# A middle stage in the source's order: attention work as a plan of single-engine steps at set k-tiles

## The chip, the cores and the metric

The kernel runs on one core of a Trainium2 chip. Its engines are TensorE (PE; its weight loads are listed apart, as PEld), VectorE (DVE), ScalarE (ACT), GpSimd (POOL) and SyncE (SP, which here only issues DMAs). Each engine works through its own list of instructions in order and waits at semaphores for the others. The metric is the time of the whole kernel on the device, in microseconds, as a median of several runs.

## What is computed

One decoder layer on 256 tokens of width 4096, all in float32. The reference, cut:

```python
h = _rmsnorm(x, norm_g[l])
proj = h @ w_in[l]
(q_a, k_a, v_a, z_a, q_b, kc, vc, ksl, vsl, kwn, vwn, z_b, g_b) = jnp.split(proj, ...)
o_a = _dilated_mixture(heads(q_a, 16) * HEAD_DIM ** -0.5, heads(k_a, 16), heads(v_a, 16), slopes_a)
gates = jax.nn.sigmoid(g_b).reshape(B, S, N_HEADS_B, 3)
o_b = _nsa(heads(q_b, 16), ..., gates, slopes_b, cmp_k_pe[l], cmp_k_w1[l], ...)
y_a = _rmsnorm(o_a, out_g_a[l]) * jax.nn.silu(z_a)
y_b = _rmsnorm(o_b, out_g_b[l]) * jax.nn.silu(z_b)
x = x + jnp.concatenate([y_a, y_b], axis=-1) @ w_out[l]
return _rmsnorm(x, final_g)
```

Mixer A is a windowed attention with three dilations and an ALiBi penalty, 16 heads of 128. Mixer B is an attention with three gated branches (compressed, selected, window), 16 heads over two groups of keys and values; its compressed keys and values come from a small two-layer network (`_compress`).

## The kernel before

Float32 products are made from two parts of each factor: a high part (`wh`, `xh`) and the rest (`wl`, `xl`). `mm3` issues three matmuls for one product: high by high, low by high, high by low (lines 97, 98, 99). `split_to` makes the parts, the high one on ScalarE (line 104) and the low one on VectorE (line 105), which needs the high one first.

The kernel has five stages. A first stream of weight chunks (to about 205 us); then `run_pairs` over the chunks of q, k, v of mixer A and q of mixer B, which are evicted to DRAM by DMAs of GpSimd's queue (`scr_q`, `scr_k`, `scr_v`, `scr_qb`), to about 853 us; then the middle stage, which the change rewrites, to about 1361 us; then `run_pairs` over most of the output projection, and a last stream.

The middle stage is one call of `run_stream` over eight chunks of 512 columns: seven gate chunks (z of both mixers) and the first chunk of `w_out`. A chunk has 32 k-tiles of 128 rows, and a k-tile six matmuls of 512 columns into `acc`. A weight DMA brings four k-tiles (`w`); they are split in halves of two k-tiles, two halves ahead of the matmuls (`LOOK`). Beside this stream the attentions run as background tasks, generators in the list `tasks`: `attend_a` (four head groups of mixer A), `compress` (keys, then values), `mixer_done`, `start_b`, `attend_b` (four head groups, each in two halves of 128 queries, `attend_half`; the second half has twice the keys and is called the larger one here), later `turn_y` and `sum_y`. After each k-tile `run_stream` adds a pace of 1.45 (1.3 in the last chunk) to a credit, and for each whole credit `advance` runs one generator to its next yield; such a step may issue a whole chain across the engines. That settles only the order of the source: `ordered.close()` at line 357 leaves the manual schedule, so that the tile framework's scheduler orders each engine's instructions, and the stage of `run_pairs` afterwards enters it again (line 1341).

Names in the rows: `fetched` is a tile read back from DRAM (`fetch`, two buffers), `table` the ALiBi table of a head of mixer A (`load_table`, line 649, GpSimd's queue, three buffers), `cmat` the distances of mixer B. In mixer A, `s` are scores, `n` table minus scores, `mn` its minima, then the exponentials in `n`, `pt` transposes, `pah` and `pal` their parts, `po` the product with the values. In mixer B, `nb` holds a half's scores of four heads, `den` the denominators, which are inverted and multiplied by the gates (lines 1007 and 1009) and then into `nb` (line 1012, four heads); `turn` (line 1047) transposes a block of 128 keys of four heads into `pt`, which becomes `pbh` and `pbl`; `c` is the compressed branch; `oT` turns a half's result. `sz` are the gates z, with Silu on ScalarE. ScalarE loads a table when its function changes (ACT_TABLE_LOAD).

Of the kernel before, what the change touches and what calls it, by code (L numbers as in the profile page):

```python
# [82 lines left out]
def hybrid_trunk(ctx: ExitStack, tc: tile.TileContext, a: dict):  # L83
# [234 lines left out]
    def run_stream(begin=None, last=False, ordered=None):  # L318
# [6 lines left out]
        for i, (u, s) in enumerate(subs):  # L325
# [49 lines left out]
            for j in range(n):  # L375
                k = k0 + n * s + j
                for m in range(NT):
                    h, l = lhs(k, m)
                    mm3(ps[m][:, :width], h, l, wh[:, j], wl[:, j], start=(k == 0), stop=(k == KT - 1))
                if k == KT - 1:  # L380
                    done(ps)
                if (c, k) in hooks:
                    hooks[c, k]()
                credit = min(credit + pace * width / CW, 2.0)
                while credit >= 1.0 and tasks:
                    credit -= 1.0
                    advance()
# [201 lines left out]
    def split_values(src):  # L589

        v = room["work"].tile([P, NT, 4, 2, HD], F32R, name="va", tag="n", bufs=2)
        for m in range(NT):
            split_to(v[:, m, :, 0], v[:, m, :, 1], src[:, m].rearrange("p (j d) -> p j d", j=4))
        return v

    def transposed(src, key, scale=None):

        if key == "ka":
            hl = room["work"].tile([P, 2, 4, SEQ], F32R, name="kaT", tag="n", bufs=2)
            h, l = hl[:, 0], hl[:, 1]  # L600
        else:
            h = room["work"].tile([P, 4, SEQ], F32R, name=key + "Th", tag="qTh", bufs=1)
            l = room["work"].tile([P, 4, SEQ], F32R, name=key + "Tl", tag="qTl", bufs=1)
        for pair in range(2):
            pt = room["psm"].tile([P, 2, NT, P], F32, name="pt", tag="ps")
            for j in range(2):
                for m in range(NT):
                    hh = 2 * pair + j
                    nc.tensor.transpose(pt[:, j, m], src[:, m, hh * HD : (hh + 1) * HD], ident)
            split_to(h[:, 2 * pair : 2 * pair + 2].rearrange("p a b -> p (a b)"),  # L610
                     l[:, 2 * pair : 2 * pair + 2].rearrange("p a b -> p (a b)"),
                     pt.rearrange("p a b c -> p (a b c)"), scale)
            yield
        st[key + "T"] = (h, l)

# [13 lines left out]
    def split_psum(pt, n, nm):  # L629
        h = room["work"].tile([P, CW], F32R, name=nm + "h", tag="pTh", bufs=2)  # L630
        l = room["work"].tile([P, CW], F32R, name=nm + "l", tag="pTl", bufs=2)
        split_to(h[:, :n], l[:, :n], pt[:, :n])
        return h, l

    def pipeline(units, stages, at):

        for t in range(len(units) + at[-1]):
            for f, d in reversed(list(zip(stages, at))):
                if 0 <= t - d < len(units):
                    f(units[t - d])  # L640
            yield
            yield
# [8 lines left out]
    def attend_a(hg):  # L651
        vsrc, qsrc = st.pop("va"), st.pop("qa")
        v = split_values(vsrc)
        ksrc = fetch(f"k{hg}")
        yield
        yield from transposed(qsrc, "qa", SCALE)
        yield from transposed(ksrc, "ka")
        if hg == 1:
            st["kvc"] = fetch("kvc")
        elif hg < 3:  # L660
            st["va"], st["qa"] = fetch(f"v{hg + 1}"), fetch(f"q{hg + 1}")
        else:
            st["sel"], st["kw"] = fetch("sel"), fetch("kw", 2 * HD)
        qh, ql = st["qaT"]
        kh, kl = st["kaT"]
        o_tiles("a")
# [3 lines left out]
        def scores(j):  # L670
            s = room["psm"].tile([P, SPAN], F32, name="s", tag="ps")
            mm3(s[:, :P], qh[:, j, :P], ql[:, j, :P], kh[:, j, :P], kl[:, j, :P])
            mm3(s[:, P:], qh[:, j, P:], ql[:, j, P:], kh[:, j], kl[:, j])
            n = room["zq"].tile([P, SPAN], F32, name="n", tag="zt", bufs=4)
            head = hg * 4 + j
            nc.vector.tensor_sub(n, tables.pop(head), s)
            load_table(head + 2)
            mn = room["work"].tile([P, NT], F32, name="mn", tag="mn", bufs=4)
            den = room["work"].tile([P, NT], F32, name="den", tag="den", bufs=4)
            for m in range(NT):  # L680
                nc.vector.tensor_reduce(mn[:, m : m + 1], n[:, parts[m]], axis=AX.X, op=OP.min)
            for m in range(NT):
                nc.scalar.activation(n[:, parts[m]], n[:, parts[m]], AF.Exp, bias=mn[:, m : m + 1], scale=-1.0,
                                     accum_out=den[:, m : m + 1])
            rden = room["work"].tile([P, NT], F32, name="rden", tag="rden", bufs=4)
            nc.vector.reciprocal(rden, den)
            live[j] = (n, rden)

        def turn(j):
            n, rden = live[j]  # L690
            pt = room["psm"].tile([P, SPAN], F32, name="pt", tag="ps")
            for b in range(3):
                nc.tensor.transpose(pt[:, b * P : (b + 1) * P], n[:, b * P : (b + 1) * P], ident)
            live[j] = (*split_psum(pt, SPAN, "pa"), rden)

        def values(j):
            ph, pl, rden = live.pop(j)
            head = hg * 4 + j

            po = room["pso"].tile([P, NT, 2, HD], F32, name="po", tag="po")  # L700
            for m, blocks in enumerate([[(0, 0)], [(P, 0), (2 * P, 1)]]):
                out = po[:, m].rearrange("p s d -> p (s d)")
                for at, b in blocks:
                    vb = v[:, b, j].rearrange("p s d -> p (s d)")
                    nc.tensor.matmul(out, ph[:, at : at + P], vb, start=b == 0, stop=False)
                    nc.tensor.matmul(out, pl[:, at : at + P], vb, start=False, stop=b == m)
            oh = o_at("a", head * HD, HD)
            nc.scalar.activation(oh, po[:, :, 0], AF.Copy)
            nc.vector.tensor_add(oh, oh, po[:, :, 1])
# [3 lines left out]
        yield from pipeline(range(4), [scores, turn, values], [0, 1, 2])  # L713
        square_sums("a", hg)

    def square_sums(which, hg):
        for m in range(NT):
            junk = room["zq"].tile([P, CW], F32, name="junk", tag="zt", bufs=4)
            nc.scalar.activation(junk, o_at(which, hg * CW, CW)[:, m], AF.Square,
                                 accum_out=o_sb["ss" + which][:, m, hg : hg + 1])  # L720
# [11 lines left out]
    waiting, finished, gated = {"a": [], "b": []}, set(), set()  # L732

    def gate(which, i, sz=None):
        r = o_sb["r" + which]
        if sz is None:
            sz = []
            for m in range(NT):
                sz.append(room["zq"].tile([P, CW], F32, name="sz", tag="zt", bufs=4))
                nc.sync.dma_start(sz[m], scratch(f"z{which}{i}")[:, m])  # L740
            yield
            yield
# [677 lines left out]
```

## Time and profile before

| what | us |
|---|---|
| median of 3 runs | 1676.73 |
| lowest and highest | 1673.76, 1678.68 |
| the profiled execution | 1672.55 |
| its span in the trace | 1670.8 |
| TensorE busy in it | 1625.5 |
| TensorE's weight loads | 1340.3 |
| VectorE, ScalarE, GpSimd busy | 1330.9, 1016.3, 148.0 |

The mean granted clock of TensorE in this execution is 0.991. A row of the timeline has the start, the time of the instructions, engine and line, what is written and read, how many (x4), and in brackets the idle time of the engine before it with what ended it. Matmuls overlap, so that the time of one is longer than the distance of two.

### The profile page before, as it was taken

The page shows a single profiled execution, that of the slowest core. Times are in us where ns is not written, and L with a number is a line of the kernel's source. Part 1 is how long each engine was busy: PE and PEld are TensorE (multiplying, and loading weights), DVE is VectorE, ACT ScalarE, POOL GpSimd, SP SyncE. Part 2 cuts the span into 40 slices and gives each one's busy share as a digit, 9 for nine tenths or more (in the row PEclk, how much of TensorE's full clock was granted, in tenths as well). Part 3 has the DMA queues.
Part 4 walks back from the last instruction along what each step waited for, and adds up shares of the span by engine and source line. Part 5 has one row for each costly group of instructions (what it writes and reads, how often), then busy time and mean ns, then how long its engine had stood idle before and what let it go on. Part 6 is the DMA issues. An engine that isn't in the chain of part 4 may idle for free.

```text
span 1670.8 us, 20883 instructions
## 1 busy us (share of the span) xinstructions
PE 1625.5 (97%) x7772; PEld 1340.3 (80%) x7772; DVE 1330.9 (80%) x1446; ACT 1016.3 (61%) x1355; POOL 148.0 (9%) x203
## 2 busy tenths in 40 slices
PE   8999999999999999999978999999999999999997
PEld 5888978788888888888867877777888878878887
DVE  6586699989898998989846777876676859898984
ACT  6675556566656565656536757866666745656554
POOL 0000001111111110202030000000000000111110
PEclk9999999999999999999989999999999999999999
DMA  9785756979797888879796665534345456898974
GB/s 355 282 319 172 239 194 218 278 246 269 249 262 245 268 249 251 265 237 273 239 296 211 252 254 181 198 139 141 130 172 208 166 199 202 231 270 244 300 281 173
DMA packets 103542, 390.78 MB, mean 234 GB/s; under 512 B 12496, under 2 KB 13136, under 8 KB 90000
## 3 DMA queue, kind: packets, MB, share of 16 engines
q1 hardware_dynamic: 80064, 336.22, 57.3%
q0 software_dynamic: 22944, 52.18, 14.1%
q8 instruction: 61, 1.00, 0.2%
q10 hardware_dynamic: 432, 1.05, 0.2%
q14 instruction: 41, 0.34, 0.1%
HBM read 341.11 MB, written 50.38 MB: 234 GB/s over the span
## 4 chain that ended last, share of the span: by engine, by line
PE 86%; DVE 6%; DMA 3%; issue 3%; ACT 2%; POOL 0%; ACTq 0%; POOLq 0%; SPq 0%; DVEq 0%
PE p L98 14%; PE p L99 14%; PE p L97 14%; PE acc L98 11%; PE acc L99 10%; PE acc L97 10%; PE e L99 2%; PE e L97 2%; PE e L98 2%; DVE bf L458 2%; DMA scr_qb<-parts 1%; DMA w<-in_w_in 1%; PE pt L1047 1%; DVE bf L457 1%; DVE bt L451 1%
## 5 line engine op out<-in xcount | busy, mean ns | idle before, releaser
L105 DVE TENSOR_TENSOR wl<-w,wh 128x1024 fp32r<-128x1024 f32 (+2 forms) x210 | 247.2, 1180 | 147.7 <-ACT wh L104 144.9
L104 ACT ACTIVATE wh<-w 128x1024 fp32r<-128x1024 f32 (+2 forms) x210 | 214.1, 1023 | 140.4 <-PE acc L99 125.9
L97 PE MATMUL acc<-wh,xh 128*128 128x512 f32 (+2 forms) x768 | 294.2, 384 | 3.9 <-ACT wh L104 3.8
L98 PE MATMUL acc<-wl,xh 128*128 128x512 f32 (+2 forms) x768 | 291.9, 380 | 1.8 <-DVE wl L105 1.8
L99 PE MATMUL acc<-wh,xl 128*128 128x512 f32 (+2 forms) x768 | 291.1, 379 | 0.0
L458 DVE TENSOR_TENSOR bf<-bt,bf 128x2048 fp32r<-128x2048 f32 x99 | 226.2, 2284 | 0.0
L453 ACT ACTIVATE bf<-bt 128x1024 fp32r<-128x1024 f32 x99 | 104.9, 1060 | 163.2 <-DVE bt L451 163.1
L105 DVE TENSOR_TENSOR bp<-bw,bp 128x2048 fp32r<-128x2048 f32 x66 | 151.0, 2288 | 63.7 <-ACT bp L104 63.7
L450 ACT ACTIVATE bf<-bw 128x1536 fp32r<-128x1536 f32 x99 | 147.0, 1485 | 68.9 <-DMA bw<-in_w_in 46.7
L457 DVE TENSOR_TENSOR bf<-bw,bf 128x1536 fp32r<-128x1536 f32 x99 | 173.4, 1751 | 0.0
L104 ACT ACTIVATE bp<-bw 128x2048 fp32r<-128x2048 f32 x66 | 126.1, 1911 | 76.7 <-PE e L99 62.4
L97 PEld LDWEIGHTS acc<-wh,xh 128*128 128x128 f32 x768 | 145.4, 190 | 28.5 <-ACT wh L104 5.7
L98 PEld LDWEIGHTS acc<-wl,xh 128*128 128x128 f32 x768 | 145.9, 190 | 26.5 <-DVE wl L105 3.4
L99 PEld LDWEIGHTS acc<-wh,xl 128*128 128x128 f32 x768 | 145.4, 189 | 24.8
L456 ACT ACTIVATE bf<-bt 128x1024 fp32r<-128x1024 f32 x99 | 105.3, 1063 | 39.6 <-DVE bt L455 38.0
L451 DVE TENSOR_TENSOR bt<-bw 128x1024 f32<-128x1024 f32 x99 | 120.9, 1222 | 10.2 <-DMA bw<-in_w_in 7.0
L98 PE MATMUL p<-bf,sum 128*128 128x512 f32 x288 | 113.1, 393 | 2.6 <-DVE bf L458 2.5
L97 PE MATMUL p<-bf,sum 128*128 128x512 f32 x288 | 112.3, 390 | 0.0
L99 PE MATMUL p<-bf,sum 128*128 128x512 f32 x288 | 112.2, 390 | 0.0
L98 PE MATMUL p<-bp,xh 128*128 128x512 f32 x288 | 112.1, 389 | 0.0
L97 PE MATMUL p<-bp,xh 128*128 128x512 f32 x288 | 112.0, 389 | 0.0
L99 PE MATMUL p<-bp,xl 128*128 128x512 f32 x288 | 112.0, 389 | 0.0
(330 smaller groups left out, 3279.2 us busy)
## 6 DMA issues: line engine op xcount, KB each, us to landing
bw<-in_w_in SPq DMA_DIRECT2D x256, 512.0 KB, 6.4
w<-in_w_in SPq DMA_DIRECT2D x76, 1024.0 KB, 5.0
bw<-in_w_out SPq DMA_DIRECT2D x96, 512.0 KB, 5.4
w<-in_w_out SPq DMA_DIRECT2D x16, 1024.0 KB, 4.9
scr_q<-parts POOLq DMA_DIRECT2D x30, 256.0 KB, 7.7
scr_k<-parts POOLq DMA_DIRECT2D x30, 256.0 KB, 7.6
scr_v<-parts POOLq DMA_DIRECT2D x30, 256.0 KB, 7.7
scr_qb<-parts POOLq DMA_DIRECT2D x30, 256.0 KB, 7.5
```

The source lines that it names most:

```text
L97: nc.tensor.matmul(out, lh, rh, start=start, stop=False)
L98: nc.tensor.matmul(out, lh, rl, start=False, stop=False)
L99: nc.tensor.matmul(out, ll, rh, start=False, stop=stop)
L104: nc.scalar.activation(h, src, AF.Copy)
L105: nc.vector.tensor_sub(l, src, h.bitcast(F32))
L450: nc.scalar.activation(h[:, :3], w[:, B22:], AF.Copy)
L451: nc.vector.tensor_tensor(t[:, T3 : T1 + 1], w[:, B22 : B11 + 1], w[:, B12 : B12 + 1].to_broadcast([P, 2, CW]), op=OP.subtract)
L453: nc.scalar.activation(h[:, 3:5], t[:, T3 : T1 + 1], AF.Copy)
L456: nc.scalar.activation(h[:, 5:], t[:, T2:], AF.Copy)
L457: nc.vector.tensor_sub(l[:, :3], w[:, B22:], h[:, :3].bitcast(F32))
L458: nc.vector.tensor_sub(l[:, 3:], t, h[:, 3:].bitcast(F32))
L1047: nc.tensor.transpose(pt[:rows, j], src, ident)
```

## The change

The manual schedule is kept through the middle stage: `ordered` is no argument of `run_stream` any more, and each engine gets its instructions in the order in which the source issues them. The generators are replaced by a heap, `plan`, of steps with a time in k-tiles of the stage. Each step issues work for one engine mostly. `run_plan` runs after each k-tile what has become due.

```diff
@@ run_stream @@
-    def run_stream(begin=None, last=False, ordered=None):
+    def run_stream(begin=None, last=False):
...
             if i == 0 and begin:
                 begin()
-                if ordered:
-                    ordered.close()
...
                 if (c, k) in hooks:
                     hooks[c, k]()
+                clock[0] += width / CW
+                run_plan()
...
+    def at(time, f, *args):
+        heapq.heappush(plan, (time, len(planned), f, args))
+        planned.append(time)
...
+    def run_plan():
+        while plan and plan[0][0] <= clock[0]:
+            run_next()
...
     def load_table(head):
         if head < NH:
-            tables[head] = room["work"].tile([P, SPAN], F32, name="table", bufs=3)
-            nc.gpsimd.dma_start(tables[head], a["consts"][:, N_TAB + head * SPAN : N_TAB + (head + 1) * SPAN])
...
+            tables[head] = room["work"].tile([P, SPAN], F32, name="table", bufs=2)
+            nc.sync.dma_start(tables[head], a["consts"][:, N_TAB + head * SPAN : N_TAB + (head + 1) * SPAN])
...
+        plan_turns(when, q, 0, SCALE)
+        if hg == 0:
+            when(0, values_high, v)
+            when(1, values_low, v)
+            when(2, get, k)
+            when(3, get, following[0])
+            plan_turns(when, k, 8)
...
+        for j in range(4):
+            for d, f in enumerate((scores, maxima, weights, turn, high, low, values, first_half, both_halves, divide)):
+                when(t0 + 4 * j + d, f, j)
...
+    def plan_gates(when, which, t, *ids):
+        for n in range(0, len(ids), 2):
+            when(t, get_gates, which, *ids[n : n + 2])
+        for n, i in enumerate(ids):
+            when(t + 6, silu, which, i)
+            when(t + 7 + n, gate, which, i)
...
         for j in range(4):
+            for i in range(len(cuts)):
+                when(2 * j + i, scores, j, i)
+                when(2 * j + i + 1, distances, j, i)
+            when(2 * j + len(cuts), maxima, j)
+            when(2 * j + len(cuts) + 1, weights, j)
+        t = 8 + len(cuts)
...
+        when(t + 0.2, gate_weights)
+        for j in range(4):
+            when(t + 0.3 + 0.5 * (j // 2), weigh, j)
...
+        step = 2 if m else 3
+        t += 1.5
+        for i in range(len(blocks)):
+            for d, f in enumerate((turn, high, low, values)):
+                when(t + step * i + d, f, i)
...
         open_b()
+        get("v0")
+        get("q0")
+        load_table(0)
+        load_table(1)
         cmat = room["work"].tile([P, N_TAB], F32, name="cmat", bufs=1)
...
-        st["va"], st["qa"] = fetch("v0"), fetch("q0")
-        load_table(0)
-        load_table(1)
-        tasks.extend([attend_a(0), attend_a(1), compress(0), compress(1), attend_a(2), attend_a(3), mixer_done("a"), start_b()]
-                     + [attend_b(hg) for hg in range(4)] + [mixer_done("b")])
-
-    pace = 1.45
...
+        plan_attentions()
...
+                when(38, mixer_done, "a")
+                plan_gates(when, "a", 38, 0, 1, 2, 3)
...
+    RATE_A, RATE_C, RATE_B = 0.75, 0.6, 1.0
...
-    run_stream(begin_rest, ordered=ordered)
-    while tasks:
-        advance()
+    run_stream(begin_rest)
+    while plan:
+        run_next()
...
-    ordered.enter_context(tc.manual_schedule())
     rest = run_pairs(a["w_out"], dcs, y_lhs, y_sops, begin_out, OUT_PLACES, OUT_BANKS, out=True)
```

A rate turns steps into k-tiles: 0.75 for mixer A, 0.6 for the compression, 1.0 for mixer B. The compression takes keys and values together; head groups follow one another at fixed distances (a half of mixer B every 10 or 11 k-tiles). In mixer B the compressed block is now the last of a half. Gates of mixer A that were computed before their mixer was done come back for Silu in one go. The sums of y are planned 1.5 k-tiles apart in the last chunk.

Three places in the order of the instructions follow. The lines of the two kernels differ by the text that was added (`split_to` is at 104 and 105 before, at 105 and 106 now; `fetch` at 577 and 578).

GpSimd at the start of the stage, before: `scr_qb` are evictions of the last pairs, `c` the memset of the compressed weights' tile.

```order
L478 DMA scr_qb_5825<-parts 128x512 x2
L478 DMA scr_qb_5824<-parts 128x512 x2
L478 DMA scr_qb_5825<-parts 128x512
L1289 MEMSET c_5960 128x384
L649 DMA table<-in_consts 128x384 x11
```

SyncE at the same place, now: `w` are weights of the stage, `scr_v`, `scr_q` and `scr_k` the first head group's values, queries and keys.

```order
L274 DMA w<-in_w_in 128x2048 x3
L578 DMA fetched<-scr_v_3290 128x1024
L578 DMA fetched<-scr_q_2308 128x1024
L626 DMA table<-in_consts 128x384 x2
L1510 DMA cmat<-in_consts 128x800
L274 DMA w<-in_w_in 128x2048
L578 DMA fetched<-scr_k_2782 128x1024
```

The tables have moved from GpSimd's queue, behind the evictions, to SyncE's, between the fetches and `cmat`; two of them are issued at once.

TensorE at the first transposes (`pt<-ident,nb`) of the first larger half of mixer B, before:

```order
L97 MATMUL acc<-wh,xh_104 128x512
L98 MATMUL acc<-wl,xh_104 128x512
L99 MATMUL acc<-wh,xl_105 128x512
L1090 MATMUL pt<-ident,oT 128x128 x4
L1047 MATMUL pt<-ident,nb 128x128 x2
L97 MATMUL acc<-wh,xh_104 128x512 x2
L1047 MATMUL pt<-ident,nb 128x128 x2
L98 MATMUL acc<-wl,xh_104 128x512
L99 MATMUL acc<-wh,xl_105 128x512
```

TensorE at the same transposes, now:

```order
L98 MATMUL s<-kBh,qTh 128x272
L99 MATMUL s<-kBl,qTh 128x272
L100 MATMUL s<-kBh,qTl 128x272
L98 MATMUL acc<-wh,xh_253 128x512
L99 MATMUL acc<-wl,xh_253 128x512
L100 MATMUL acc<-wh,xl_254 128x512
L98 MATMUL acc<-wh,xh_253 128x512
L99 MATMUL acc<-wl,xh_253 128x512
L100 MATMUL acc<-wh,xl_254 128x512
L1274 MATMUL pt<-ident,oT 128x128 x4
L1241 MATMUL pt<-ident,nb 128x128 x4
L98 MATMUL acc<-wh,xh_253 128x512
```

The transposes no longer stand in pairs between the matmuls of a k-tile, but as four in a row at its end.

VectorE where the `nb` of this half are weighed, before:

```order
L1007 RECIPROCAL den<-den 128x8
L1009 TENSOR_TENSOR den<-den,gates 128x4 x2
L1012 TENSOR_TENSOR nb<-nb,den 128x2x256 x2
L105 TENSOR_TENSOR wl<-w,wh 128x1024
L1012 TENSOR_TENSOR nb<-nb,den 128x2x256 x2
L1022 TENSOR_REDUCE dc<-nb 128x4
L105 TENSOR_TENSOR wl<-w,wh 128x1024
```

VectorE at the same products, now (`mc` and `dc` belong to the compressed branch, `qTl` to the next head group's queries):

```order
L106 TENSOR_TENSOR wl<-w,wh 128x1024
L1203 TENSOR_REDUCE mc<-nb 128x4
L1204 SCALAR_TENSOR_TENSOR nb<-mc,nb 128x4x16
L658 SCALAR_TENSOR_TENSOR qTl<-pt,qTh 128x512
L1190 RECIPROCAL den<-den 128x8
L1192 TENSOR_TENSOR den<-den,gates 128x4 x2
L1196 TENSOR_TENSOR nb<-nb,den 128x2x256 x4
L658 SCALAR_TENSOR_TENSOR qTl<-pt,qTh 128x512
L106 TENSOR_TENSOR wl<-w,wh 128x1024
```

In this half a `wl` stood between the products (in the other larger halves all four stood together already); now the four stand together behind a `wl` and the half's small work, with the next `wl` behind them.

ScalarE at the first gates of mixer A, before:

```order
L719 ACTIVATE junk,ssa<-o_a_6056 128x512 x2
L104 ACTIVATE wh<-w 128x1024
L744 ACT_TABLE_LOAD
L744 ACTIVATE sz<-sz 128x512 x4
L104 ACTIVATE wh<-w 128x1024 x3
L744 ACTIVATE sz<-sz 128x512 x2
```

ScalarE at the gates of mixer A, now:

```order
L105 ACTIVATE wh<-w 128x1024
L799 ACT_TABLE_LOAD
L799 ACTIVATE sz_8016<-sz_8016 128x512 x4
L799 ACTIVATE sz_8019<-sz_8019 128x512 x4
L1248 ACTIVATE pbh<-pt 128x512
L1222 ACTIVATE c_5957<-nb 128x4x16 x2
L1185 ACT_TABLE_LOAD
L1185 ACTIVATE nb,den<-nb,mn 128x256 x2
L105 ACTIVATE wh<-w 128x1024
```

Before, six Silus stand in a four and a two with three `wh` between them; now eight stand together, with one table load ahead of them and one behind.

## Rows read from the trace of the kernel before

**Rows 1.** TensorE's waits: engine, tile, line, releaser: us in total, times, longest.

```profile
PE pt L693 <- ACT n L683: 11.0, 1, 11.0
...
PE pt L609 <- DMA fetched<-scr_k: 4.1, 1, 4.1
...
PE ph L869 <- DVE bhl L105: 1.3, 2, 0.7
...
PE pt L1090 <- ACT oT L1086: 1.0, 1, 1.0
```

**Rows 2.** Stretches: length, busy PE, PEld, DVE, ACT, POOL (instructions), clock, DMA share, GB/s.

```profile
850.00:890.00 40.00, 24.86 (x113) 20.55 (x111) 12.16 (x21) 12.59 (x26) 11.46 (x17) 0.79 0.91 253
890.00:1060.00 170.00, 166.67 (x908) 134.54 (x908) 125.74 (x210) 120.25 (x243) 7.16 (x15) 1.00 0.65 230
1060.00:1240.00 180.00, 178.04 (x915) 144.04 (x914) 132.06 (x278) 117.85 (x271) 0.00 (x0) 1.00 0.41 143
1240.00:1360.00 120.00, 120.00 (x564) 99.63 (x563) 79.82 (x112) 74.82 (x110) 1.98 (x3) 1.00 0.55 193
```

**Rows 3.** Timeline of SyncE and GpSimd: start, us, issues at the stage's start.

```profile
848.47 0.37 SPq L577 DMA_DIRECT2D fetched<-scr_q  x1
...
874.91 1.91 POOL L649 DMA_DIRECT2D table<-in_consts  x3
```

**Rows 4.** Timeline of VectorE and ScalarE at the first head.

```profile
880.48 0.56 DVE L676 TENSOR_TENSOR n<-table,s 128x384 f32<-128x384 f32 x1 [11.84 <-DMA table<-in_consts]
...
882.28 1.04 ACT L104 ACTIVATE wh<-w 128x1024 fp32r<-128x1024 f32 x1
```

**Rows 5.** Stretches as in Rows 2, chosen by the clock (third from the end).

```profile
862.00:867.60 5.60, 5.59 (x17) 4.63 (x18) 1.48 (x2) 2.14 (x3) 1.93 (x3) 0.50 1.05 309
...
1376.30:1379.60 3.30, 3.30 (x10) 2.58 (x9) 3.27 (x3) 0.39 (x1) 0.00 (x0) 0.53 0.62 211
```

**Rows 6.** Timeline of TensorE, matmuls of 256 and 512 columns in a row.

```profile
869.03 0.28 PE L99 MATMUL s<-kaT,qaTl 128*128 128x256 f32 x1
869.15 0.40 PE L97 MATMUL acc<-wh,xh 128*128 128x512 f32 x1
869.39 0.40 PE L98 MATMUL acc<-wl,xh 128*128 128x512 f32 x1
```

**Rows 7.** Timeline of VectorE and ScalarE in attention B, smaller half first.

```profile
1118.42 1.43 DVE L1012 TENSOR_TENSOR nb<-nb,den 128x256 f32<-128x256 f32 x4
...
1126.56 0.76 DVE L998 SCALAR_TENSOR_TENSOR nb<-cmat,s 128x256 f32<-128x256 f32 x2
1127.23 0.68 DVE L1001 TENSOR_REDUCE mn<-nb 128x2 f32<-128x512 f32 x1
...
1131.33 0.49 ACT L1003 ACTIVATE nb<-nb,mn 128x256 f32<-128x256 f32 x1
...
1131.46 1.23 DVE L105 TENSOR_TENSOR wl<-w,wh 128x1024 fp32r<-128x1024 f32 x1 [1.07 <-ACT wh L104]
...
1133.10 2.50 DVE L1012 TENSOR_TENSOR nb<-nb,den 128x512 f32<-128x512 f32 x4
```

**Rows 8.** DMA issues: transfer, queue, times, KB each, us from issue to landing.

```profile
w<-in_cmp_k_w SPq DMA_DIRECT2D x4, 1024.0 KB, 6.9
```

**Rows 9.** Timeline of TensorE at the first transposes of a larger half.

```profile
1133.85 0.44 PE L1047 MATMUL pt<-ident,nb 128*128 128x128 f32 x2
1134.04 0.47 PE L99 MATMUL acc<-wh,xl 128*128 128x512 f32 x1
```

**Rows 10.** Timeline of ScalarE at a Silu.

```profile
1080.82 1.28 ACT L762 ACT_TABLE_LOAD   x1
1082.12 0.60 ACT L762 ACTIVATE sz<-acc 128x512 f32<-128x512 f32 x1
```

**Rows 11.** Timeline of TensorE behind the stage, in the output pairs.

```profile
1373.69 0.50 PE L98 MATMUL p<-bf,yh 128*128 128x512 f32 x1 [1.49 <-DVE bf L457]
...
1375.90 0.51 PE L98 MATMUL p<-bf,ysum 128*128 128x512 f32 x1 [1.25 <-DVE bf L458]
```

More of the change, by code (lines that the diff above doesn't have):

```diff
@@ L1 @@
+import heapq
 import math
@@ L627, in o_at, with run_next @@
         return o_tiles(which)[q][:, :, at : at + n]
[L629 to L642, printed above, removed]
+    plan = []
+    clock = [0.0]
+    def at(time, f, *args):
+        heapq.heappush(plan, (time, len(planned), f, args))
+        planned.append(time)
+    planned = []
+    def run_next():
+        _, _, f, args = heapq.heappop(plan)
+        f(*args)
+    def run_plan():
+        while plan and plan[0][0] <= clock[0]:
+            run_next()
     tables = {}
@@ L710, in values, with both_halves, divide @@
+        def both_halves(j):
+            oh = o_at("a", (hg * 4 + j) * HD, HD)
+            nc.vector.tensor_add(oh, oh, live.pop(("po", j))[:, :, 1])
+        def divide(j):
+            oh, rden = o_at("a", (hg * 4 + j) * HD, HD), live.pop(("den", j))
             for m in range(NT):
                 nc.scalar.activation(oh[:, m], oh[:, m], AF.Copy, scale=rden[:, m : m + 1])
[L713 to L720, printed above, removed]
+        for j in range(4):
+            for d, f in enumerate((scores, maxima, weights, turn, high, low, values, first_half, both_halves, divide)):
+                when(t0 + 4 * j + d, f, j)
@@ L730, in hybrid_trunk, with get_gates, silu, gate @@
     yh, yl, turned = [None] * 4, [None] * 4, set()
[L732 to L742, printed above, removed]
-            for m in range(NT):
-                nc.scalar.activation(sz[m], sz[m], AF.Silu)
+    finished, gated = set(), set()
+    gates_in = {}
+    def get_gates(which, *ids):
+        t = room["o"].tile([P, 2, NT, CW], F32, name="sz2", tag="o", bufs=4) if which == "a" else None
+        for n, i in enumerate(ids):
+            if t is None:
+                z = fetch(f"z{which}{i}")
+            else:
+                z = t[:, n]
+                nc.sync.dma_start(z, scratch(f"z{which}{i}"))
+            gates_in[which, i] = [z[:, m] for m in range(NT)]
+    def silu(which, i):
+        for sz in gates_in[which, i]:
+            nc.scalar.activation(sz, sz, AF.Silu)
+    def gate(which, i):
+        r, sz = o_sb["r" + which], gates_in.pop((which, i))
         for m in range(NT):
@@ new lines, in plan_compress @@
+        gelu = (halves, turn_halves, gelu_in, gelu_inner, gelu_tanh, gelu_out)
+        when(-6, load_w1, 0)
+        when(-4, load_w1, 1)
+        when(-5, load_small, 0)
+        for c in range(2):
+            when(c, turn, c)
+            when(c + 1, keep, c)
+        when(2.5, get, "k2")
+        for c, t in ((0, 3), (1, 20)):
+            for d, f in enumerate((blocks, blocks_high, blocks_low)):
+                when(t + d + (c if d else 0), f, c)
+            when(t + 13, load_w2, c)
+            when(t + 19, second_high, c)
+            when(t + 20, second_low, c)
```

758 lines of the change are left out of this document (443 added, 315 removed).

## The prediction

> **What bounds the kernel now.** TensorE does. I read the list of TensorE's waits first, then the engines' busy time by stretch, then the timeline where a wait stands. TensorE counts as busy nearly all the time, but matmuls overlap and a stretched one still counts, so the better measure is the time of its weight loads. From 1240 to 1360 us, with little but full-width matmuls, loads take 99.63 of 120 us, a share of 0.83: the ceiling [rows 2]. The changed stage runs from about 853 to 1361 us. From 890 to 1060 us (attention A and the compression) loads take 134.54 of 170 us, where the ceiling would be 141.1: 6.6 us of loads, 7.9 us of time. From 1060 to 1240 us (attention B) they take 144.04 of 180, where it would be 149.4: 6.5 us of time [rows 2]. The attentions' small matmuls have another share of loads, so these deficits are upper bounds of what an order could win there. The waits that the trace names there are small, 1.3 and 1.0 us the largest entries [rows 1].
>
> The stage's first 40 us are another matter. Two waits stand there, 11.0 us for an exponential and 4.1 us for fetched keys [rows 1]. The first goes back to the first ALiBi table: its DMA is issued on the GpSimd queue at 874.91 us, behind the last evictions of the pairs' results and a memset [rows 3]; VectorE, idle for 11.84 us until it lands, subtracts at 880.48, and the exponential that TensorE waits for comes behind that [rows 4]. Behind the other wait, from 862.0 to 867.6 us, TensorE runs at the lower of its two clock levels, 0.50 [rows 5].
>
> **The change, part by part.** The sum is made against the profiled execution of 1672.55 us, which lies 4.2 us below the median of 1676.73; the 4.2 us are added back at the end.
>
> *The start, -17.* The first two tables move from the GpSimd queue, behind the evictions, to SyncE's, behind the fetch of q0, which now leaves at 848.47 us [rows 3]. So they leave some 26 us earlier, and the 11.0 us wait goes. The fetch of k0 waits there for a buffer that q0's last transposes free; by the planned times it is issued about 5 k-tiles into the stage and needed after 9. A k-tile is six matmuls at the 0.24 us that separate two of 512 columns, or 1.4 us [rows 6]; so 5 to 6 us lie between. The 4.1 us wait shrinks to about 1 us: bounds 0 (it lands in time) and 4.1 (late as now). With the wait goes the half-clock stretch, half of 5.6 us [rows 5]. Together 11.0 + 4.1 + 2.8 = 17.9, less 1: -17, bounds -18 and -11 (a wait of 4.1 left, and its clock with it). Next late is nothing that the trace shows: VectorE and ScalarE were idle there [rows 2, 4].
>
> *Attention A and the compression, -2.* Each head becomes ten steps on set k-tiles (one step is 0.75 k-tile, about 1 us). Between a head's scores and its transposes lie three steps, 3.1 us and small matmuls, and what runs there, from the subtraction's start to the wh pass that follows the exponentials, is 1.8 us [rows 4], behind at most one wl pass of 1.2 [rows 7]. That is just covered. The tables' new queue is SyncE's, where 16 small DMAs now stand between the weight loads; each waits for a minimum of two heads before, long done by then. The compression weights land after 6.9 us [rows 8], and the plan gives them some 3 k-tiles, 4 to 6 us with small matmuls: 1 to 3 us late at a load that nothing else delays, up to 5 us lost in all. Bounds -8 (the whole deficit goes) and +5; I take -2, about what the named waits of that stretch come to, with a few smaller entries beside that of 1.3 [rows 1].
>
> *Attention B, +7.* Here set places cost something. In every one of the eight half head groups the softmax weights are multiplied by gates and reciprocals on VectorE (den, then four products) and then transposed on TensorE. In the old order these transposes stand between the single matmuls of the k-tile, two at a time, and TensorE never waits [rows 9]. In the new one four transposes stand in a block behind whole k-tiles, and VectorE does the products behind a wl pass, whose wh pass on ScalarE waits for a free buffer, that is for the end of a k-tile. From that end: wh 1.04 [rows 4], wl 1.23, reciprocals about 0.4, products 2.50 in the larger half and 1.43 in the smaller [rows 7]: 5.2 and 4.1 us. TensorE has 2 k-tiles and one or two scores to do meanwhile, 3.1 to 3.6 us. So it waits 1.6 to 2.1 us in the four larger halves and 0.5 to 1.0 in the four smaller: 8.4 to 12.4, say 10. Second, in the larger halves a score step costs ScalarE and VectorE in turn: two exponentials 0.98 (0.49 each), wh 1.04, wl 1.23, distances 0.76, minimum 0.68 [rows 4, 7]: 4.7 us, against 2 k-tiles, two scores (six matmuls of 0.12 us [rows 6]) and one product with the values, 4.2 us. Eight such steps at 0.5: 4 us. Third, mixer A's eight Silus (0.60 each) now come in one block with a table load of 1.28 us ahead and one behind, 7.4 us in front of the next wh [rows 10]; two to three k-tiles with small work, 4 to 5.6 us, cover it. So 2 to 4 us, say 3. Sum 10 + 4 + 3 = 17. These waits follow one another, and each lets ScalarE and VectorE run ahead as far as three weight buffers allow, so a later one is smaller: I keep four fifths, 13.5. Off goes the old deficit of 6.5: +7. Bounds: -6 (as good as a full stretch) and +16 (no wait hides another, and the score matmuls wait for a PSUM buffer on top, 5 us as an estimate from two products of 2.50 [rows 7]).
>
> *The first output chunk, +1.* Its sums of y move to fixed places; at the ceiling already [rows 2], it can only lose. A sum costs VectorE about as much as 1.5 k-tiles offer beside wl: bounds 0 and +3.
>
> *At nothing.* Four of seven table loads of ScalarE go, 4 x 1.28 = 5 us [rows 10], beside TensorE. The matmuls stay as many; from 1361 us on the order is the old one.
>
> At the table loads the Trainium skill has another price (ScalarE: Activation LUTs, What ACT_TABLE_LOAD costs): a switch is said to cost a drain of 1.38 us on top of the load. Here the Silu starts 1.30 us after its load started [rows 10], so no drain shows at this switch; by the page's figure the block of Silus would, as an estimate, be 2.8 us longer and attention B as much worse.
>
> Sum: -17 - 2 + 7 + 1 = -11. 1672.55 - 11 = 1661.5, and with the 4.2 us 1666.
>
> **The rivals.** *Slower: the waits of B win.* One mechanism: VectorE's products behind wl in the eight halves. No wait hides another (17), the PSUM buffer adds 5, and the waits stand close enough that the clock falls. The trace shows such a fall: waits of 1.49 and 1.25 us within 3 us, and just behind them, from 1376.3 us, the clock is 0.53 for 3.3 us, which costs half of that, 1.6 us [rows 11, 5]. Against it: the single 1.0 us wait of B [rows 1] left the clock of its stretch at 1.00 [rows 2]. With six such falls: 17 + 5 + 10 - 6.5 = +25 for B; with -13 at the start, A at 0 and +1: +13, 1690. It decides from where B costs some 3 us per half more than now, 23 in all (with -17, -2 and +1 to be made up and 5 left over).
>
> The Trainium skill has this as a rule (TensorE: Matmul & The Clock Gate, A second HAM failure mode: psum-queue depth-cycling): frequent short idle times between groups of matmuls make the clock fall and rise again, and the cost is that. The rows of the kernel before bear it out at one place only; by the rule the time is this rival's.
>
> *Larger gain: a hand order without waits.* If B wins half of its deficit (-3), A its whole 8 and the start 18: -28 with +1 for the output chunk, 1649. For it: VectorE and ScalarE are busy 73 and 65% of 1060 to 1240 us [rows 2], so there is room. Against it: the chain above, whose pieces stand in one queue.
>
> *Same: the start's wait comes back elsewhere.* SyncE's queue holds tables, fetches and weight loads in order, and each can hold those behind it. If a late k0 or weight tile costs 8 of the 17 us, A wins nothing and B is as forecast: -9 + 0 + 7 + 1 = -1, 1676. Against it: the DMA engines move 230 GB/s from 890 to 1060 us at a share of 0.65 [rows 2].
>
> **How the numbers follow.** Forecast (1656 to 1672) 0.47, larger gain (1643 to 1656) 0.16, same (1672 to 1682) 0.17, slower (1682 to 1700) 0.20. About 0.3%, 5 us, can be told from no change. Faster than 1671.7: 0.47 + 0.16 less a little, 0.62; slower than 1681.8: 0.20; the rest, 0.18, within. The range runs from 1647 (the larger gain, nearly whole) to 1686 (most of B's upper bound, few falls of the clock); about 0.1 is left out on either side.
>
> **What would show it.** The 11.0 us wait for the first exponential should be gone, the first table's DMA should be issued before 855 us, and the first 40 us should show weight loads of 31 us or more, where they show 20.55 [rows 2]. B should show TensorE's waits for VectorE's products at the first transposes of each half, 1 to 2 us in the larger halves, and one wait of 2 to 4 us for wh behind the Silus. I am wrong if these transposes don't wait, if the load share of B rises, if the granted clock of B falls below 1.00, or if the start keeps a wait above 4 us.

## The result, and the profile after

The changed kernel takes 1691.65 us (median of 4 runs, 1690.75 to 1692.70), the kernel before 1675.24 us (4 runs, 1673.21 to 1678.68): a ratio of 1.0096, 95% interval 1.0076 to 1.0116. It is slower by 16 us, where I had forecast 11 us faster. The profiled execution has 1692.48 us and a span of 1690.6, 19.8 more than before.

Where the time went can be cut at four matmuls. By their starts in the two traces, the first matmul of the input pairs comes at 193.5 us (199.1 before), so 5.6 us are won in the first stream. From the first to the last of the 1536 `acc` matmuls the middle stage takes 532.1 us (508.0 before): 24.1 lost. The pairs before it and all behind it differ by about 1 us each.

TensorE's waits in the stage, after (columns as in Rows 1):

```profile
PE s L98 <- DVE nb L1173: 5.7, 4, 2.7
PE ph L972 <- DVE o_a L754: 5.2, 1, 5.2
PE po L747 <- DVE pal L736: 4.6, 5, 1.7
PE ph L973 <- DVE w1hl L959: 4.1, 5, 2.1
PE po L99 <- DVE pbl L1253: 3.7, 5, 1.4
PE pt L727 <- ACT n L720: 3.7, 9, 1.1
PE s L100 <- DVE qTl L658: 3.2, 2, 1.8
PE pv L100 <- DVE rhl L1045: 3.1, 1, 3.1
PE pt L1241 <- ACT o_b L1277: 2.6, 3, 1.2
PE pt L639 <- DVE qTl L658: 2.6, 2, 1.3
...
PE pt L1241 <- DVE nb L1196: 1.1, 5, 0.3
```

The two waits at the head of [rows 1] are gone. In their place stand many, most of 0.5 to 2 us, nearly all for VectorE. All entries of the stage come to 41.8 us, before to 19.5, of which 15.1 were the two at the start.

The stretches after (columns as in Rows 2):

```profile
850.00:890.00 40.00, 38.78 (x207) 32.52 (x206) 24.36 (x39) 22.47 (x45) 7.34 (x10) 1.00 0.88 241
890.00:1060.00 170.00, 147.18 (x794) 120.97 (x793) 107.51 (x182) 100.87 (x205) 0.00 (x0) 0.96 0.57 207
1060.00:1260.00 200.00, 182.98 (x921) 146.94 (x920) 140.83 (x284) 121.45 (x281) 0.72 (x1) 1.00 0.41 149
1260.00:1380.00 120.00, 118.59 (x562) 97.43 (x561) 78.14 (x114) 76.58 (x117) 4.77 (x7) 1.00 0.58 211
```

Against [rows 2]: the first 40 us now hold 32.52 us of weight loads instead of 20.55. From 890 to 1060 us the share of loads has fallen from 0.79 to 0.71, in attention B from 0.80 to 0.73. VectorE is less busy from 890 to 1060 us than before (107.51 against 125.74 us), and yet TensorE waits for it. Time is not what it lacks; the experiments ask whether it is the order.

One such wait, in the timeline after:

```profile
924.89 0.41 DVE L754 TENSOR_TENSOR o_a<-o_a,po 128x256 f32<-128x256 f32 x1
925.00 1.02 ACT L945 ACTIVATE bhl<-bt 128x960 fp32r<-128x960 f32 x1 [0.93 <-DVE bt L940]
...
925.92 1.04 ACT L105 ACTIVATE wh<-w 128x1024 fp32r<-128x1024 f32 x1
...
926.99 1.23 DVE L106 TENSOR_TENSOR wl<-w,wh 128x1024 fp32r<-128x1024 f32 x1 [1.70 <-ACT wh L105]
...
928.14 0.55 DVE L736 TENSOR_TENSOR pal<-pt,pah 128x384 fp32r<-128x384 f32 x1
...
928.74 0.39 PE L747 MATMUL po<-va,pal 128*128 128x256 f32 x1 [1.05 <-DVE pal L736]
```

VectorE is done with `o_a` at 925.3 us and idle for 1.70 us. The next in its list is `wl`, which needs `wh`; on ScalarE `wh` stands behind `bhl`, which had waited for VectorE. `pal`, whose input `pah` had been ready since 924.1 us, stands behind `wl`, comes 2.8 us later than it could, and TensorE waits 1.05 us. None of these steps waits for a transfer; the `wh` before them, at 920.53 us, had waited 1.15 us for its weights.

The largest wait, 5 us further on:

```profile
930.60 0.36 ACT L750 ACTIVATE o_a<-po 128x256 f32<-128x256 f32 x1
930.86 1.05 ACT L105 ACTIVATE wh<-w 128x1024 fp32r<-128x1024 f32 x1
931.94 1.23 DVE L106 TENSOR_TENSOR wl<-w,wh 128x1024 fp32r<-128x1024 f32 x1 [1.05 <-ACT wh L105]
933.08 1.22 DVE L959 TENSOR_TENSOR w1hl<-w,w1hl 128x1024 fp32r<-128x1024 f32 x1
934.22 0.41 DVE L754 TENSOR_TENSOR o_a<-o_a,po 128x256 f32<-128x256 f32 x1
...
934.78 0.44 PE L972 MATMUL ph<-w1hl,bhl 128*60 128x256 f32 x1 [5.18 <-DVE o_a L754]
```

The compression's product `ph` takes the one PSUM buffer that the last head's `po` held, and `po` is free when VectorE has read it (`o_a`, 0.41 us). That small step was possible from 931.0 us; it ran at 934.22, behind two long passes.

SyncE's queue is in order too, and weights stand in it behind evictions of gates and behind tables that wait for VectorE. SyncE's waits in the stage, and ScalarE's for late weights:

```profile
SPq L829 <- ACT sz L823: 70.2, 10, 19.9
SPq L626 <- DVE mn L713: 60.4, 14, 7.9
```

```profile
ACT wh L105 <- DMA w<-in_w_in: 17.3, 8, 4.8
```

Before, and in the changed kernel with the scheduler, no `wh` of the stage waits for weights. So late weights are one more rival, which no run tests by itself.

### The profile page after: what moved, and what is told of

It reads as the page before. It is cut to its first block, busy times and chain, and to the rows that moved or that the text cites. A ratio compares the mean times of both kernels' runs of the same rounds, so it can differ in the third digit from the quotient of the medians.

```text
span 1690.6 us, 20844 instructions
## 1 busy us (share of the span) xinstructions
PE 1625.8 (96%) x7772; PEld 1340.9 (79%) x7772; DVE 1331.4 (79%) x1445; ACT 1012.5 (60%) x1354; POOL 137.7 (8%) x185
## 3 DMA queue, kind: packets, MB, share of 16 engines
q10 hardware_dynamic: 432, 1.05, 0.2%
## 4 chain that ended last, share of the span: by engine, by line
PE 72%; DVE 13%; ACT 6%; DMA 5%; issue 4%; POOL 0%; SPq 0%; ACTq 0%; POOLq 0%; DVEq 0%
PE p L99 13%; PE p L100 13%; PE p L98 13%; PE acc L99 8%; PE acc L100 8%; PE acc L98 8%; DVE wl L106 3%; ACT wh L105 2%; PE e L100 2%; PE e L98 2%; PE e L99 2%; DVE bf L459 2%; DMA bw<-in_w_in 1%; DMA w<-in_w_in 1%; DVE bf L458 1%
## 5 line engine op out<-in xcount | busy, mean ns | idle before, releaser
L454 ACT ACTIVATE bf<-bt 128x1024 fp32r<-128x1024 f32 x99 | 104.9, 1060 | 174.8 <-DVE bt L452 174.8
```

Source lines behind the costliest of these rows:

```text
L454: nc.scalar.activation(h[:, 3:5], t[:, T3 : T1 + 1], AF.Copy)
```

## The experiments

The theory after the result: the fixed order is at fault. Each engine takes its steps strictly in the source's order, and a step that TensorE needs soon stands behind a wl or wh pass that can't run yet. Its rivals: the planned times are too tight, whoever orders them; the chains on ScalarE or the PSUM buffers hold; late weights hold `wh`; and the gain at the start wasn't real.

**The tables alone, in the kernel before.**

```diff
-            nc.gpsimd.dma_start(tables[head], a["consts"]...)
+            nc.sync.dma_start(tables[head], a["consts"]...)
```

> The kernel before with one edit: the ALiBi tables are loaded on SyncE's queue instead of GpSimd's; the scheduler and the generators stay. If the wait at the start of the stage comes from the tables' place in GpSimd's queue alone, the 11.0 us wait goes and the run is 11 to 17 us faster than before, about 1660 us. If the start is set by something else (the fetch of k0, the scheduler's order), less than 5 us are gained.

Measured: 1663.69 us, before 1674.73 (ratio 0.9934, 0.9916 to 0.9953). 11 us, as the wait was long. The fetch of k0 still comes late there, in TensorE's waits from 850 to 890 us:

```profile
PE pt L609 <- DMA fetched<-scr_k: 4.6, 1, 4.6
```

In the changed kernel k0 is fetched in time too, and that list names neither of the two. So the gain at the start is real.

**The plan with the scheduler.**

```diff
             if i == 0 and begin:
                 begin()
+                if ordered:
+                    ordered.close()
...
-    run_stream(begin_rest)
+    run_stream(begin_rest, ordered=ordered)
...
+    ordered.enter_context(tc.manual_schedule())
     rest = run_pairs(a["w_out"], ...)
```

> The changed kernel with the scheduler back: the manual schedule is left at the start of the stage and entered again at the output pairs, while the plan of steps stays. Theory order: the waits of the stage (some 67 us of excess over the usual distances of matmuls, against 49 before) come from each engine taking its steps strictly in the source's order behind the wh and wl passes, so with the scheduler they fall to 35 us or less and the run takes about 1660 us. Rival plan: the planned times are too tight for the chains whoever orders them; then the run stays within 6 us of the changed kernel, 1686 to 1697 us.

Measured: 1647.99 us (ratio to before 0.9840, 0.9820 to 0.9859). 44 us less than the changed kernel with the same steps, times and buffers, and 12 us better than expected. TensorE's waits in its stage:

```profile
PE pv L98 <- ACT rhl L1043: 2.4, 1, 2.4
PE ph L974 <- DVE o_a L756: 1.6, 1, 1.6
PE ph L974 <- ACT w1hl L956: 1.5, 1, 1.5
PE pt L729 <- ACT n L722: 0.6, 3, 0.3
PE acc L99 <- DVE wl L106: 0.3, 1, 0.3
```

6.4 us are left of 41.8. The wait for `po`'s buffer is still there, with 1.6 instead of 5.2 us: here `o_a` runs directly behind the passes that were ready. The rival of too tight times falls: 1686 us was its lower end. ScalarE's chains fall as well: it has 21 table loads in the stage here, 3 in the changed kernel.

What VectorE loses at the head of its list, in the changed kernel and with the scheduler (85.0 us before):

```profile
DVE wl L106 <- ACT wh L105: 161.4, 93, 9.3
```

```profile
DVE wl L106 <- ACT wh L105: 75.0, 69, 2.7
```

**Splitting one half unit ahead.**

```diff
-                elif n_sp < len(subs) and n_sp <= i + LOOK and subs[n_sp][0] < n_st:
+                elif n_sp < len(subs) and n_sp <= i + look[0] and subs[n_sp][0] < n_st:
...
     room["first"] = False
+    look[0] = 1
```

> The changed kernel with the weights of the middle stage and what follows split one half unit ahead instead of two, with the same three buffers, so that a wh pass never waits for TensorE to free a buffer. Theory order, in the form that the wait of wh for TensorE is what holds the steps behind it: waits of the stage fall by 10 us or more, 1680 us or less. Rival: the steps ahead of wh hold wh itself, and TensorE then waits for wh and wl directly: 1695 us or more.

Measured: 1678.00 us (10 runs; ratio to before 1.0026, 1.0015 to 1.0036), 13.6 us less than the changed kernel. `wh` waits 5.3 us for TensorE where it waited 63.8, and 2.5 us for weights where it waited 17.3; the run doesn't tell the two apart, and together they are about a third of the cost. The wait for TensorE costs only through what stands behind it: with the scheduler it is as long, 64.7 us. TensorE's waits for wl rise to 3.1 us in five pieces, which is the price that the rival had named, and it is small.

**Without the low parts of the weights.**

```diff
-            split_to(h[:, j : j + w], l[:, j : j + w], t[...])
+            if nowl[0]:
+                nc.scalar.activation(h[:, j : j + w], t[...], AF.Copy)
+            else:
+                split_to(h[:, j : j + w], l[:, j : j + w], t[...])
```

> The changed kernel with the low parts of the stage's weights left out: VectorE does no wl pass there (128 of 1.23 us), and the product takes wh in its place. Theory order: with no wl ahead of them VectorE's steps come on time, and the stage loses its waits but for some 15 us of excess: 1645 us or less. Rival chain: ScalarE's passes, PSUM buffers and the length of the chains hold it, and it stays above 1675 us.

Measured: 1644.54 us in one run. TensorE's waits in the stage come to 10.1 us, and its first three lines are:

```profile
PE s L98 <- DVE nb L1177: 4.6, 1, 4.6
PE ph L976 <- DVE o_a L758: 3.1, 1, 3.1
PE pt L731 <- ACT n L724: 1.6, 2, 1.5
```

With no wl in VectorE's list the fixed order costs hardly more than the scheduler's order with it (488.1 us of stage against 483.7). The first line stands at the block of Silus, behind a `wh` that waits 5.5 us for its weights. The run alone could mean too much work on VectorE; but with the scheduler the same work, wl and all, fits with few waits. The two together point at wl's place; that is an inference, as no run keeps wl and moves nothing else. Late weights are not the main cost: here `wh` still waits 19.1 us for them, and TensorE waits 10.1.

**The scheduler in one half of the stage.**

```diff
# scheduler in attention A and the compression (left at the stage's start, as above), then
+        at(now - 3.0, lambda: ordered.enter_context(tc.manual_schedule()))
         for hg in range(4):
             for m in range(NT):
...
# fixed order there, the scheduler from attention B on
+        at(now - 3.0, lambda: ordered.close())
```

> The changed kernel with the scheduler ordering attention A and the compression (from the start of the stage), and the source's order from 3 k-tiles before attention B to the end. The scheduler over the whole stage took 44 us off the changed kernel (1648 against 1692). By the excess over the usual distances of matmuls, attention A and the compression hold about half of what the fixed order costs. Theory additive: 15 to 25 us come back here, 1667 to 1677 us. Rival: nearly all of the loss stands in attention B, where I had put it; then 5 us or less come back, 1687 us.

> The other half: the changed kernel with the source's order in attention A and the compression and the scheduler from 3 k-tiles before attention B to the end of the stage. Theory additive: what the run before gives and what this one gives add up to the 44 us; 19 to 29 us come back, 1663 to 1673 us. Rival: the loss is attention B's, 35 us or more come back, 1657 us or less.

Measured: 1668.55 us (1665.73 to 1671.58, 8 runs; ratio to before 0.9966, 0.9956 to 0.9976) and 1677.71 us (1674.97 to 1680.73, 10 runs; 1.0018, 1.0007 to 1.0029). That is 23 and 14 us back, 37 of 44; the second lies short of the 19 us expected at least. Of the 7 us that the sum is short, 2 stand in the first stream: against the changed kernel the pairs start 5.9 us later in the second kernel, 4.2 us later with the scheduler throughout, and no later in the first. 3 stand in the stage, and the rest is within the spread of the runs. The stage alone shows it, by starts of its first and last `acc` matmul, beside all of TensorE's waits in it:

```
kernel                                  stage us   waits us
before                                  508.0      19.5
changed                                 532.1      41.8
changed, scheduler                      483.7       6.4
changed, scheduler in A                 507.0      22.5
changed, scheduler in B                 511.7      24.8
changed, split one ahead                515.5      28.4
changed, no wl                          488.1      10.1
changed, split a k-tile later           524.5      33.9
```

25.1 and 20.4 us, together 45.5 of 48.3: the two halves add up, and attention A with the compression holds the larger part. The last columns go together: against the changed kernel, a microsecond of waits goes with 1.0 us of the stage (split a k-tile later) to 1.4 us (scheduler, no wl).

**Splitting a k-tile later.**

```diff
-                elif n_sp < len(subs) and n_sp <= i + LOOK and subs[n_sp][0] < n_st:
+                elif n_sp < len(subs) and n_sp <= i + LOOK - late[0] and subs[n_sp][0] < n_st:
...
                 run_plan()
+                if late[0] and j == 0 and n_sp < len(subs) and n_sp <= i + LOOK and ...:
+                    split_unit(*subs[n_sp])
+                    n_sp += 1
```

> The changed kernel with one edit of its fixed order: the wh and wl passes of the next half unit are issued one k-tile later, behind the first k-tile of a half unit and its steps instead of ahead of them, so that their buffer is free by then and the steps of the first k-tile stand ahead of them. Theory order (steps late because they stand behind a wl whose wh waits for TensorE): most of the 16 us that the look-ahead of one gave back, or more, 1665 to 1678 us. Rival (steps too many for the time, whatever stands first): 1686 us or more.

Measured: 1683.17 us (1680.56 to 1683.91; ratio to before 1.0047, 1.0029 to 1.0065). Between the two: 8.5 us back, where I had expected 14 at the least. The place of wl by hand in one pattern for the whole stage isn't enough. `wh` waits only 2.8 us for weights here, and TensorE still waits 33.9 us: with weights nearly on time most of the loss stays.

**The products with the gates, a k-tile of room.**

```diff
         step = 2 if m else 3
-        t += 1.5
+        t += 2.5
```

> The changed kernel with the transposes of a half of mixer B and all that follows them in the half planned one k-tile later behind the products with the gates. By the prediction's largest term (10 us of waits for these products) 7 us or more come back, 1685 us or less. By the trace of the changed kernel, where the transposes wait only 1.1 us for the products in all, less than 4 us move, to either side.

Measured: 1691.04 us in one run, 0.6 less than the changed kernel, which is within the spread. These waits fall from 1.1 to 0.2 us, and those of the same transposes for `o_b` from 2.6 us to none; but the scores' waits for `nb` rise from 5.7 to 8.6 us, and the clock falls three times in attention B. So the room is paid for elsewhere. The prediction's largest term, 10 us, measures 1.1.

**Without the block of Silus.**

```diff
-            when(t + 6, silu, which, i)
+            if which == "b":
+                when(t + 6, silu, which, i)
```

> The changed kernel without the eight Silus of mixer A that stand in one block (mixer A is gated by z itself). By the prediction this block costs 2 to 4 us; in the trace of the changed kernel TensorE's waits next to it come to about 6 us: 1684 to 1687 us. If the waits there come from the gates' products on VectorE and not from the Silus, 3 us or less are gained.

Measured: 1688.13 us in one run, 3.5 us less (the changed kernel's runs spread over 2); less than the trace's 6 us, and near the 3 us of the prediction. Waits for `nb` (PSUM buffers of scores) fall from 5.7 to 3.1 us. The rest stands there without the Silus as well, and so does a `wh` that waits 4.8 us for its weights just ahead of them.

**The residual copies late, in the kernel before.**

```diff
         nc.gpsimd.memset(B["c3"].bitcast(F32), 0.0)
+        for c in range(1, 5):
+            nc.gpsimd.dma_start(scratch(f"r{c}"), a["x"][...])
...
-        for c in range(1, 5):
-            nc.gpsimd.dma_start(scratch(f"r{c}"), a["x"][...])
```

> The kernel before with one edit: the four copies of the residual to DRAM, which the scheduler puts at the very beginning of GpSimd's list, are issued in the part with a fixed order, behind the last evictions of the input pairs. In the changed kernel they stand late as well, and its first 40 us have 27.2 us of weight loads where before has 23.2. If the copies compete with the first loads, this run is 4 to 6 us faster than before, about 1670 us; if the difference of the first 40 us has another cause, it is the same as before.

Measured: 1677.59 us (11 runs; ratio 1.0019, 1.0009 to 1.0029): 2 us slower, not the 4 to 6 faster that were expected; but the two parts can be told apart in the trace. The input pairs start at 193.5 us as in the changed kernel, 5.7 earlier than before. And the copies now stand ahead of the tables on GpSimd's queue, so that the wait at the stage's start has grown by 10.2 us:

```profile
PE pt L693 <- ACT n L683: 21.2, 1, 21.2
```

**Two versions with both.**

```diff
# a_best: the plan with the scheduler, and the four copies in the fixed part, at the start of the stage
# a_best2: the plan with the scheduler up to the first output chunk:
     def before_out():
+        ordered.enter_context(tc.manual_schedule())
```

> The plan with the scheduler in the middle stage, and the four residual copies issued in the part with a fixed order. Theory: the 44 us of the scheduler and the 4 to 6 us of the first stream add up, 1643 us. Rival: the copies at the start of the middle stage delay its tables and weights and take that back, 1648 us or more.

> The plan with the scheduler in the attentions' part, and the source's order again from the first output chunk, so that the four residual copies are not taken to the start of the program. Theory: the scheduler's 44 us and the first stream's 5 us add up, 1642 to 1645 us. Rival: the source's order in the first output chunk costs what the first stream gains, 1648 us.

Measured: 1649.04 us (1647.04 to 1650.39; ratio to before 0.9848, 0.9835 to 0.9862) and 1646.23 us (1643.47 to 1647.57; 0.9828, 0.9813 to 0.9844). Both start the pairs at about 193 us. The first gives it back at the stage's start: its second 16 k-tiles take 39.1 us against 33.4 with the scheduler alone, and 4.4 us of a new wait for an exponential stand there. The second gives most of it back in the stage, 488.6 us against 483.7, with 3.3 us of waits for wl and wh where the scheduler leaves 0.3. Against the scheduler alone (1647.99) 2 us can't be told from none; neither theory's time was clearly reached. All three beat both kernels, by 26 to 28 us the one before.

## Why the prediction was wrong, point by point

**The start, -17: right in its mechanism.** Both waits of [rows 1] and the half-clock stretch of [rows 5] are gone; the first 40 us hold 32.52 us of loads, where I had asked for 31. The tables alone are worth 11 us by a run; no run measures the rest by itself. The 12 us of loads are 14 us of time at the ceiling of 0.83, so the size lies between 14 and my 18. A second half-clock stretch, behind the 11.0 us wait, was missing in my sum; in the trace before:

```profile
881.90:884.70 2.80, 2.77 (x12) 2.57 (x13) 1.51 (x3) 1.81 (x4) 0.09 (x1) 0.50 0.25 70
```

**Attention A and the compression, -2: this step failed.** The named waits from 890 to 1060 us went from 2.8 to 22.6 us. By the prediction's own measure, loads against the ceiling of 0.83, the deficit of these 170 us is 24 us where it was 7.9: +16, not -2. The scheduler takes 25 us off the stage there. The sum had set 3.1 us of room against a chain of 1.8 us [rows 4] behind "at most one wl pass of 1.2". What I left out is that wl waits for wh, and wh for ScalarE's own list and for a buffer: `pal` above came 2.8 us late for a pass of 1.23. I had used just this argument for attention B and not for A. The compression's weights, for which I had allowed 5 us, are not named in any of these waits; its cost is the shared PSUM buffer (5.2 us), `w1hl` (4.1) and `rhl` (3.1 and 0.5), most of it behind VectorE's list: 12.9 of the 22.6 us, where the heads' own `pal` and `n` have 7.1. Wrong as well was that the tables' minima are "long done by then": SyncE's queue waits 60.4 us for them, with weights behind.

**Attention B, +7: right in sign, too small, and its main term was wrong.** By loads against the ceiling B's deficit is 23 us where it was 6.5: +16.5 against my +7. (The 20 us that the scheduler gives back there are counted from the plan, not from before.) The products with the gates, 10 of my 17 us, wait 1.1 us in all, and that the transposes don't wait was one of my signs of being wrong. I had let all four products end before the first transpose. In the trace they end between 0.15 us ahead of its start and 1.66 us behind it: each transpose needs one product only, and TensorE waits 0.3 us at the most. The Silus' 3 us came out at 3.5, but TensorE waits there for `nb`, not for `wh`. The scores' wait for a PSUM buffer, which VectorE's distances free, stood in my upper bound alone, at 5 us; it measures 5.7 in four pieces, part of it at the Silus. What I had no term for are `qTl` (3.2 us; 2.6 more before attention B), `pbl` (3.7) and `o_b` (2.6, at the first transposes): like the distances, steps of 0.4 to 0.7 us that stand behind something longer. Whether one wait makes the next smaller, as my four fifths assumed, no run shows.

**The output chunk, +1.** Loads of 97.43 us in 120 against 99.63: 2 to 3 us, within the bounds of 0 to 3.

**Missing: the first stream, -5.6.** Before, the scheduler takes the four residual copies, which depend on nothing, to the start of the program. The rows of the first 40 us, before and after, and GpSimd's timeline before:

```profile
0.00:40.00 40.00, 33.66 (x124) 23.21 (x125) 24.28 (x42) 24.04 (x41) 3.04 (x8) 0.96 0.93 364
0.00:40.00 40.00, 38.16 (x148) 27.19 (x149) 28.41 (x49) 27.52 (x48) 0.20 (x4) 1.00 0.89 340
```

```profile
1.32 2.18 POOL L1322 DMA_DIRECT2D scr_r<-in_x  x3 [0.87 <-POOLq L1409]
10.58 0.66 POOL L1322 DMA_DIRECT2D scr_r<-in_x  x1 [7.08 <-issue]
```

The DMA engines are at 0.93 there, the first weights are on their way, and TensorE gets 4 us less of loads. In the fixed order the copies stand at 1289 us. In the order of GpSimd's instructions this could be seen before any run; I looked only at the stage that the change names.

**The sum.** -17 - 2 + 7 + 1 = -11 was forecast. By loads the parts are about -14, +16, +16.5 and +3, 21 of the 24 us that the stage lost. By the experiments the plan with the scheduler is 24.3 us below before (483.7 against 508.0), of which 14 to 18 are the start by the estimate above, and the fixed order is +48; with -5.6 in the first stream and some 1 us more, +20 in the profiled executions and +16 in the medians. The rival "the waits of B win" had the time, 1690, and gave it 0.20; it had the engine (VectorE, behind wl), but the wrong steps and only half of the stage, and its clock is not what happened. In B the clock stays at 1.00 through all these waits. It falls behind the single long wait of 5.2 us:

```profile
935.00:939.00 4.00, 4.00 (x14) 3.38 (x14) 1.17 (x1) 1.64 (x3) 0.00 (x0) 0.50 0.79 262
```

A fall of the same size follows the 3.1 us wait for `rhl` near 1000 us; by the distances of the matmuls the two falls cost some 4 us. The Trainium skill (TensorE: Matmul & The Clock Gate, A second HAM failure mode: psum-queue depth-cycling) puts such a fall down to frequent short idle times. In attention B this trace shows none: 20 waits of up to 2.7 us, 16.6 us in all, left the clock alone. The run that splits a k-tile later agrees with it at one place: four waits for the products, of 0.66, 0.21, 0.27 and 0.27 us within 2.4 us, have a fall right behind them.

```profile
1245.02 0.30 PE L1245 MATMUL pt<-ident,nb 128*128 128x128 f32 x1 [0.66 <-DVE nb L1200]
...
1246.74 0.33 PE L1245 MATMUL pt<-ident,nb 128*128 128x128 f32 x1 [0.27 <-DVE nb L1200]
```

```profile
1247.40:1250.80 3.40, 3.40 (x10) 2.63 (x9) 1.84 (x7) 2.25 (x6) 0.00 (x0) 0.50 0.04 14
```

So the rival's clock can happen at these products; in the changed kernel it didn't, though four waits of 0.21 to 0.28 us stand at the products near 1257 us as well.

## What to carry to other kernels

A wait on an in-order engine is paid by everything behind it: with a plan written by hand, put to each step's time not only the long pass ahead of it but what that pass itself waits for, on its own engine and on the next. A good plan of times and a fixed order are two changes; here the first took 24 us off the stage, more than half of them at its start, and the second cost 48. Where a scheduler is switched on or off, look at the whole program's order, and above all at DMAs without dependences, which can move by a millisecond.

## What I had not expected of the hardware

TensorE's waits can cost more than their length: between the changed kernel with and without the scheduler, 35.4 us of waits go with 48.3 us of the stage, which leaves 13 us for falls of the clock and for matmuls that start slowly; how much is which is not settled here. In the run that splits a k-tile later 7.9 us of waits went with 7.6 us. The length of a wait alone doesn't tell whether the clock falls: in the changed kernel it took a wait of 2.7 us and others of 1 to 2 us without a fall, and fell behind 3.1 and 5.2 us; with the scheduler it fell behind 2.4 us, with the split one ahead behind 1.9 us, and in [rows 11] behind 1.49 and 1.25 us.
